# The first stage of a two-layer backbone: a feature tile's eight modulation chunks in one run, and two engine queues in source order

## The chip, the cores and the metric

One core of one Trainium2 chip. The metric is the device time of one execution in microseconds (us), smaller is better. TensorE is called PE below, its weight loads PEld, VectorE DVE, ScalarE ACT, GpSimd POOL; SP is the engine whose queue issues the loads.

## The reference, cut to what matters

Two layers, 512 tokens (256 latent and 256 context), width 2048. Each layer begins with

```python
shift, scale, gate = jnp.split(jax.nn.silu(c) @ w_mod + b_mod, 3, axis=-1)
shift_x, scale_x, gate_x = jnp.split(jax.nn.silu(c_ctx) @ w_mod + b_mod, 3, axis=-1)
z_lat = (rms_norm(h_lat, norm_g) * (1.0 + scale[:, None]) + shift[:, None]) @ w_in
z_ctx = (rms_norm(h_ctx, norm_g) * (1.0 + scale_x) + shift_x) @ w_in
```

and goes on with three branches (a gated linear recurrence, a chunked delta rule, attention), their gates, an output projection and a gated residual. All of it is float32. The two vectors `c` and `c_ctx` are known at the start, but `w_mod` is 2048 x 6144 for each layer, so that the shift and scale of layer 0 have to be computed from 32 MB of weights before the first projection can be fed.

## The kernel before, in words

Features lie on the partitions, tokens along the columns. A feature tile is 128 features; there are 16 (`KT`), and each `Y[k]` holds one tile of the residual for all 512 tokens. A projection in full precision is made of three PE products per feature tile and output tile: both operands are split into a rounded part (`xh`, `wh`) and the rest (`xl`, `wl`), and `accumulate` (L397) issues xh*wh, xh*wl and xl*wh into one PSUM bank.

The change is in the first stage of layer 0, `start_first` (L543). Seven output tiles of the input projection (`NSTART`) are accumulated at once, in seven PSUM banks named pz, pz, pa, pa, pb, pb and pt; the loop runs over the feature tile k outside and over the seven output tiles i inside, so that one k is 21 products of 128x512. Before k can be used, its modulation must be known, and that is what class `Narrow` (L217) does for a tile u:

- `load(u)` (L228) loads the 2048 x 256 columns of `w_mod` that give shift and scale of tile u, as eight chunks in six DMAs: three 256 KB chunks into buffers wb, one into wa, one pair of 512 KB into full or th (in turn), one pair into kq. wb has eight buffers, wa four, kq two, full and th one each, so the last three DMAs of a load reuse what tile u-2 has read.
- `run(u, half)` (L241) multiplies four of the eight chunks with the two vectors: 4 x 4 matmuls with an output of 2x128, each in one of four column strips of the array, all into PSUM tile pm. The trace shows each of them as two records, so the eight chunks are 64 records. After the second half ACT copies pm to SBUF tile s.
- `end(u)` (L251) transposes s with a small matmul against a constant (pm<-sel,s), and DVE makes `modA` and `modS` from it.

`modulate` (L342) then makes u = Y * modA * rb (DVE, two halves), xh (ACT, two halves) and xl (DVE, two halves), where rb is the broadcast of the RMS norm. `first_load` (L521) loads the 448 KB of weights of the seven output tiles for one k into wraw, `first_split` (L525) makes wh (ACT) and wl (DVE) of it. One k thus loads 4 x 256 + 2 x 512 + 448 = 2496 KB.

In the source the first half of tile k+2's chunks stands after output tile 5 of step k, the second half of tile k+1's chunks after output tile 1, `end(k+1)` and `modulate(k+1)` after output tile 2. That is not the order in which PE gets them: the framework's scheduler orders each engine's instructions by its own estimate of when they are ready, and puts pieces of one and two chunks between the products. `late` (L1129, called after k = 11) loads constants that are needed only later.

After the stage, the seven results go to the branches, and `project` (L403) makes the remaining output tiles one by one; small steps of the branches and DVE's own share of the modulation products for later (macc) are put between by a planner that counts estimated engine time. pt is used next by `beta_alpha`.

Of the kernel before, what the change touches and what calls it, by code (L numbers as in the profile page):

```python
# [13 lines left out]
P = 128  # L14
KT = 16
T = 256
TT = 512
# [77 lines left out]
def trunk(ctx, tc, xT, cT, consts, masks, rope_t, small, fg, w_mod0, w_mod, w_first, w_in, w_ba, w_rg, w_out, out):  # L95
    nc = tc.nc
    pe, dve, act, pool = Timed(nc.tensor, "pe"), Timed(nc.vector, "dve"), Timed(nc.scalar, "act"), Timed(nc.gpsimd, "pool")
# [9 lines left out]
    def psum(tag, shape=(P, TT), bufs=2):  # L107
        return ps.tile(list(shape), F32, tag=tag, name=tag, bufs=bufs)
# [3 lines left out]
    def tmp(tag, shape=(P, TT), bufs=None, dt=F32):  # L112
        return wk.tile(list(shape), dt, tag=tag, name=tag, bufs=bufs or BUFS.get(tag, 2))

    def pt_():
        return psum("pt", bufs=1)

    def pa_():
        return psum("pa", bufs=2)

    def pb_():
        return psum("pb", bufs=2)
# [55 lines left out]
    def rsqrt_small(out_, in_, n, add, mul):  # L178
        dve.tensor_scalar(out=out_, in0=in_, scalar1=add, scalar2=mul, op0=ALU.add, op1=ALU.mult)
        pool.tensor_tensor(out=out_, in0=out_, in1=mhalf[:, 0:n], op=ALU.pow)  # L180
# [13 lines left out]
    def rms_bcast(sums, w, between=lambda: None):  # L194
        n = w // P
        p1 = pt_()
        for c in range(n):
            for i, a in enumerate(sums):
                pe.matmul(out=p1[:, 2 * c:2 * c + 2], lhsT=a[:, c * P:c * P + P], rhs=ones[:, 0:2], start=(i == 0), stop=(i == 1))
        r4 = tmp("r4", (P, 8))  # L200
        rsqrt_small(r4[:, 0:n], p1[:, 0:2 * n].rearrange("p (c x) -> p c x", x=2)[:, :, 0], n, 2048.0 * EPS, 1.0 / 2048.0)
        between()
        p2 = pt_()
        for c in range(n):
            pe.matmul(out=p2[:, c * P:c * P + P], lhsT=r4[:, c:c + 1].to_broadcast([P, P]), rhs=ident, start=True, stop=True)
        return p2
# [10 lines left out]
    class Narrow:  # L217
# [20 lines left out]
                w += [two[:, 0], two[:, 1]]  # L238
            self.chunks[u] = w

        def run(self, u, half):  # L241
            for j in range(4 * half, 4 * half + 4):
                for c in range(4):
                    pe.matmul(out=self.pm[32 * c:32 * c + 2, 0:P], lhsT=cs[:, 2 * j + c // 2, :], rhs=self.chunks[u][j][:, c * P:c * P + P],
                              start=(j == 0), stop=(j == 7), tile_position=(0, 32 * c))
            if half:
                self.mt = tmp("s", (P, P))
                act.copy(out=self.mt, in_=self.pm[:, 0:P])
                self.chunks.pop(u)

        def end(self, u):  # L251

# [89 lines left out]
    def modulate(l, k, rb):  # L342
        xr = tmp("u")
        xh[k] = big.tile([P, TT], F32R, tag=f"xh{k}", name=f"xh{k}")
        xl[k] = big.tile([P, TT], F32R, tag=f"xl{k}", name=f"xl{k}")
        half = [slice(T * m, T * m + T) for m in range(2)]
        for m, cc in enumerate(half):
            dve.scalar_tensor_tensor(out=xr[:, cc], in0=Y[k][:, cc], scalar=modA[l][:, k, m:m + 1], in1=rb[:, cc], op0=ALU.mult, op1=ALU.mult)
        for m, cc in enumerate(half):
            act.activation(out=xh[k][:, cc], in_=xr[:, cc], func=AF.Identity, bias=modS[l][:, k, m:m + 1])  # L350
        for m, cc in enumerate(half):
            dve.scalar_tensor_tensor(out=xl[k][:, cc], in0=xr[:, cc], scalar=modS[l][:, k, m:m + 1], in1=xh[k][:, cc].bitcast(F32), op0=ALU.add, op1=ALU.subtract)
# [44 lines left out]
    def accumulate(pz, wh, wl, c0, k, n):  # L397
        a, b = wh[:, c0:c0 + P], wl[:, c0:c0 + P]
        pe.matmul(out=pz[:, 0:n], lhsT=a, rhs=xh[k][:, 0:n], start=(k == 0), stop=False)
        pe.matmul(out=pz[:, 0:n], lhsT=b, rhs=xh[k][:, 0:n], start=False, stop=False)  # L400
        pe.matmul(out=pz[:, 0:n], lhsT=a, rhs=xl[k][:, 0:n], start=False, stop=(k == 15))
# [119 lines left out]
    def first_load(l, k):  # L521
        first_raw[k] = wp.tile([P, 1024], F32, tag="wraw", name="wraw", bufs=4)
        nc.sync.dma_start(out=first_raw[k][:, 0:P * NSTART], in_=w_first[l, k])

    def first_split(k):  # L525
        raw = first_raw.pop(k)
        first_w[k] = [split_w(raw[:, 0:512], 512), split_w(raw[:, 512:P * NSTART], P * NSTART - 512)]
# [15 lines left out]
    def start_first(acc, late):  # L543

        first = [psum("pz"), psum("pz"), pa_(), pa_(), pb_(), pb_()]
        narrow = Narrow()
        for u in range(2):
            narrow.load(u)  # L550
            first_load(0, u)
        pr = rms_bcast(acc, TT, lambda: narrow.run(0, 0))
        rb = tmp("wa")
        dve.tensor_copy(rb, pr)
        narrow.run(0, 1)
        narrow.end(0)
        modulate(0, 0, rb)
        first_split(0)
        narrow.load(2)
        first_load(0, 2)  # L560
        first.append(pt_())
        for k in range(KT):
            for i in range(NSTART):
                wh, wl = first_w[k][i // 4]
                accumulate(first[i], wh, wl, P * (i % 4), k, TT)
                if k + 1 == KT:
                    continue
                if k == 0 and i == 0:
                    narrow.run(1, 0)
                if i == 1:  # L570
                    narrow.run(k + 1, 1)
                    if k + 3 == KT - 1:
                        first_load(0, k + 3)
                    if k + 3 < KT:
                        narrow.load(k + 3)
                    if k + 3 < KT - 1:
                        first_load(0, k + 3)
                    first_split(k + 1)
                if i == 2:
                    narrow.end(k + 1)  # L580
                    modulate(0, k + 1, rb)
                if i == 5 and k + 2 < KT:
                    narrow.run(k + 2, 0)
            first_w.pop(k)
            if k == KT - 5:
                late()
        return first

    def start_layer(l, acc, bs, wide):

        first = [psum("pz"), psum("pz"), pa_(), pa_(), pb_(), pb_()]
        pr = rms_bcast(acc, TT, lambda: [mod_step(pe) for _ in range(FILL)])
        rb = tmp("wa")
        modulate(l, 0, pr)
        dve.tensor_copy(rb, pr)
        first.append(pt_())
        for k in range(KT):
            if k + 1 < KT:
                first_weights(l, k + 1)
                modulate(l, k + 1, rb)  # L600
            for i in sorted(range(NSTART), key=lambda i: wide(TILES[l][i][0])):
                wh, wl = first_w[k][i // 4]
                accumulate(first[i], wh, wl, P * (i % 4), k, TT if wide(TILES[l][i][0]) else T)
            first_w.pop(k)
        return first

    def layer(l, acc, bs):
        last = l == 1
        s = sm[l]
# [7 lines left out]
        def rope_tables():  # L617
            for dst, o in ((cq, 0), (sq_, T)):
                nc.sync.dma_start(out=dst, in_=rope_t[:, o:o + T])
                dve.tensor_scalar(out=dst, in0=dst, scalar1=s[:, S_QN:S_QN + 1], scalar2=None, op0=ALU.mult)  # L620
# [514 lines left out]
        if last:  # L1135
            rope_tables()
            first = start_layer(l, acc, bs, wide)
        else:
            first = start_first(acc, late)
        tiles = TILES[l][NSTART:]  # L1140
        groups = [[t] for t in tiles]
        weights = Weights([[w_in[l, n]] for n in range(len(tiles))] + [[w_out[l, n]] for n in range(KT)])
# [19 lines left out]
        acc = []  # L1162
# [21 lines left out]
    acc = []  # L1184
    for k in range(KT):
        square_into(acc, Y[k], k, TT, dve)
    gw = []
    acc = layer(0, acc, None)
    mod_finish(((1, 0), (1, 1)))
    acc = layer(1, acc, gw[0])  # L1190
    pr = rms_bcast(acc, T)
    rb = tmp("wa")
# [84 lines left out]
```

## Time and profile before

| | us |
|---|---|
| three runs, lowest, median, highest | 1553.96, 1554.66, 1558.1 |
| the profiled execution's own time | 1552.67 |
| its span from the first to the last instruction | 1550.9 |
| mean granted PE clock (1 is 2.4 GHz) | 0.994 |
| PE, PEld, DVE, ACT, POOL busy share of the span | 96%, 77%, 75%, 48%, 7% |

The profiled execution is 1.77 us longer than its span, and 1.99 us below the median of the three runs. Busy time of PE counts a matmul from its start to its modelled end, and these overlap; the pace of PE is read from the distance of two starts.

### The profile page before, as it was taken

The numbers are of one execution on the slowest core, as the hardware profiler recorded it, in microseconds if no ns is written. First come the engines' busy times: TensorE is split into PE (matmuls) and PEld (weight loads), VectorE is DVE, ScalarE is ACT, GpSimd is POOL, SyncE is SP. The second block draws the span as 40 slices with busy tenths as digits, with TensorE's granted clock in tenths as the row PEclk, the third lists the DMA queues.
The fourth block names the chain that finished last, engine by engine and source line by source line (L and its number), as shares of the span: only waits on it lengthen the run. The fifth ranks groups of instructions, "written<-read, shape, count | busy, mean of one in ns | idle before, by whom it ended". The sixth has DMA issues, their size and how long they took to land.

```text
span 1550.9 us, 29964 instructions
## 1 busy us (share of the span) xinstructions
PE 1482.8 (96%) x11762; PEld 1197.9 (77%) x11762; DVE 1164.5 (75%) x2513; ACT 739.3 (48%) x1708; POOL 112.2 (7%) x114
## 2 busy tenths in 40 slices
PE   4999999999999999999999999999999999999996
PEld 2555677787877887788888887967977889779996
DVE  4333888898898888999838776887895676778755
ACT  3222444554544544665422223554544556677653
POOL 0000010100020010000001110010100100000011
PEclk9999999999999999999999999999999999999998
DMA  9888354343443454344436656545662333233663
GB/s 340 286 288 297 111 166 147 97 150 123 143 150 123 150 153 136 97 143 162 135 125 212 204 194 208 174 150 164 198 188 65 96 110 102 76 110 119 194 184 116
DMA packets 90686, 247.68 MB, mean 160 GB/s; under 512 B 9200, under 2 KB 20912, under 8 KB 90544
## 3 DMA queue, kind: packets, MB, share of 16 engines
q1 hardware_dynamic: 89392, 244.71, 49.0%
q8 instruction: 92, 1.51, 0.4%
q10 hardware_dynamic: 1152, 1.05, 0.2%
q14 instruction: 50, 0.41, 0.1%
HBM read 243.60 MB, written 2.13 MB: 158 GB/s over the span
## 4 chain that ended last, share of the span: by engine, by line
PE 76%; DVE 13%; DMA 4%; ACT 4%; issue 2%; POOL 1%; SPq 0%; DVEq 0%; ACTq 0%; POOLq 0%
PE pz L89 54%; PE pa L89 9%; PE pb L89 7%; PE pt L89 3%; PE pm L89 3%; DVE wl L89 3%; DVE wb L89 2%; DVE macc L89 2%; DMA wraw<-in_w_in 1%; DVE u L89 1%; DVE th L89 1%; DMA wb<-in_w_mod 1%; ACT wb L89 1%; ACT wh L89 1%; DMA Y<-in_xT 1%
## 5 line engine op out<-in xcount | busy, mean ns | idle before, releaser
L89 PE MATMUL pz<-xh,wh 128*128 128x512 f32 (+1 forms) x1760 | 645.6, 367 | 8.6 <-ACT xh L89 8.4
L89 PE MATMUL pz<-xh,wl 128*128 128x512 f32 (+1 forms) x1760 | 630.7, 358 | 1.0 <-DVE wl L89 1.0
L89 PE MATMUL pz<-xl,wh 128*128 128x512 f32 (+1 forms) x1760 | 628.7, 357 | 0.0
L89 ACT CAST wh<-wraw 128x512 fp32r<-128x512 f32 x488 | 293.5, 612 | 336.0 <-PE pz L89 212.5
L89 DVE TENSOR_TENSOR wl<-wraw,wh 128x512 fp32r<-128x512 f32 x488 | 328.9, 682 | 134.6 <-ACT wh L89 132.8
L89 PEld LDWEIGHTS pz<-xh,wh 128*128 128x128 f32 x1760 | 331.8, 189 | 58.5 <-ACT xh L89 12.4
L89 PEld LDWEIGHTS pz<-xl,wh 128*128 128x128 f32 x1760 | 332.0, 189 | 50.0 <-issue 2.9
L89 PEld LDWEIGHTS pz<-xh,wl 128*128 128x128 f32 x1760 | 332.5, 189 | 43.2 <-DVE wl L89 1.7
L89 DVE SCALAR_TENSOR_TENSOR macc<-wm,cs,macc 128x512 f32<-128x512 f32 x400 | 293.4, 766 | 1.7 <-DMA wm<-in_w_mod 1.2
L89 PE MATMUL pb<-wb 128*128 128x128 f32 (+1 forms) x560 | 112.5, 328 | 3.9 <-ACT wb L89 2.1
L89 PEld LDWEIGHTS pb<-wb 128*128 128x128 f32 x560 | 79.6, 190 | 17.0 <-ACT wb L89 7.1
L89 DVE TENSOR_SCALAR modA<-pm,nb,small 128x2 f32<-128x2 f32 x16 | 4.5, 279 | 92.5 <-PE pm L89 92.5
L89 ACT ACTIVATE wb<-pb,mx,rqa 128x512 f32<-128x512 f32 (+1 forms) x48 | 33.9, 706 | 42.8 <-DVE mx L89 42.5
L89 POOL TENSOR_TENSOR o<-o,t 128x512 f32<-128x512 f32 (+1 forms) x28 | 30.5, 1089 | 325.6 <-ACT t L89 325.6
L89 DVE SCALAR_TENSOR_TENSOR u<-zp,small,u 128x512 f32<-128x512 f32 (+1 forms) x72 | 50.5, 702 | 2.1 <-ACT u L89 1.8
L89 ACT COPY s<-pm 128x128 f32<-128x128 f32 x16 | 4.2, 265 | 97.1 <-PE pm L89 97.1
L89 ACT ACTIVATE t<-pt 128x128 f32<-128x128 f32 (+1 forms) x122 | 34.1, 279 | 28.9 <-PE pt L89 26.8
L89 ACT ACTIVATE xh<-u,modS 128x256 fp32r<-128x256 f32 x64 | 30.5, 504 | 32.8 <-DVE u L89 32.6
L89 PEld LDWEIGHTS pa<-c,s 32*32 32x32 f32 x2304 | 24.9, 107 | 21.9 <-issue 11.9
L89 DVE TENSOR_REDUCE mx<-pb 128x1 f32<-128x512 f32 (+1 forms) x48 | 28.7, 599 | 10.2 <-PE pb L89 9.9
L89 ACT COPY wb<-pb 128x512 f32<-128x512 f32 (+1 forms) x48 | 24.7, 515 | 22.0 <-PE pb L89 21.4
L89 POOL TENSOR_TENSOR rqa<-rqa,mhalf 128x4 f32<-128x4 f32 (+1 forms) x16 | 17.3, 1083 | 243.7 <-DVE rqa L89 243.7
(260 smaller groups left out, 1811.7 us busy)
## 6 DMA issues: line engine op xcount, KB each, us to landing
wraw<-in_w_in SPq DMA_DIRECT2D x148, 512.0 KB, 3.6
wm<-in_w_mod SPq DMA_DIRECT2D x128, 512.0 KB, 3.8
wraw<-in_w_out SPq DMA_DIRECT2D x64, 512.0 KB, 4.3
wraw<-in_w_first SPq DMA_DIRECT2D x32, 448.0 KB, 5.3
wb<-in_w_mod SPq DMA_DIRECT2D x48, 256.0 KB, 6.5
kq<-in_w_mod SPq DMA_DIRECT2D x16, 512.0 KB, 5.6
Y<-in_xT SPq DMA_DIRECT2D x16, 256.0 KB, 5.3
wa<-in_w_mod SPq DMA_DIRECT2D x16, 256.0 KB, 6.7
```

What stands on the lines that cost most here:

```text
L89: return f(*args, **kw)
```

## The change

`Narrow.run` takes all eight chunks of a tile at once. Its one call per step stands after output tile 1, the calls for the first half are gone, and so is the one inside the RMS norm. `start_first` is called under `manual_schedule` for PE and SP: in that stage these two engines get their instructions in the order of the source; ACT, DVE and POOL are ordered by the scheduler as before.

```diff
-        def run(self, u, half):
-            for j in range(4 * half, 4 * half + 4):
+        def run(self, u):
+            for j in range(8):
                 for c in range(4):
                     pe.matmul(out=self.pm[32 * c:32 * c + 2, 0:P], lhsT=cs[:, 2 * j + c // 2, :], rhs=self.chunks[u][j][:, c * P:c * P + P],
                               start=(j == 0), stop=(j == 7), tile_position=(0, 32 * c))
-            if half:
-                self.mt = tmp("s", (P, P))
-                act.copy(out=self.mt, in_=self.pm[:, 0:P])
-                self.chunks.pop(u)
+            self.mt = tmp("s", (P, P))
+            act.copy(out=self.mt, in_=self.pm[:, 0:P])
+            self.chunks.pop(u)
...
-        pr = rms_bcast(acc, TT, lambda: narrow.run(0, 0))
+        pr = rms_bcast(acc, TT)
...
-        narrow.run(0, 1)
+        narrow.run(0)
...
-                if k == 0 and i == 0:
-                    narrow.run(1, 0)
                 if i == 1:
-                    narrow.run(k + 1, 1)
+                    narrow.run(k + 1)
...
-                if i == 5 and k + 2 < KT:
-                    narrow.run(k + 2, 0)
...
-            first = start_first(acc, late)
+            with tc.manual_schedule(engines={mybir.EngineType.PE, mybir.EngineType.SP}):
+                first = start_first(acc, late)
```

What it does to PE's queue around the end of step k = 1 and the begin of step k = 2 (xh_500 and xl_501 are tile 2 before, xh_502 and xl_503 after; pm<-wb, wa, th, full and kq are modulation chunks, here of tile 3, and pt, pz, pa, pb the projection's products; a row's x4 or x8 counts matmuls). Before:

```order
L89 MATMUL pt<-xh_411,wl 128x512
L89 MATMUL pm<-wb,cs 2x128 x4
L89 MATMUL pt<-xl_412,wh 128x512
L89 MATMUL pm<-wb,cs 2x128 x4
L89 MATMUL pm<-wa,cs 2x128 x4
L89 MATMUL pz<-xh_500,wh 128x512
L89 MATMUL pz<-xh_500,wl 128x512
L89 MATMUL pm<-wb,cs 2x128 x4
L89 MATMUL pz<-xl_501,wh 128x512
```

Now, the same place of PE's queue:

```order
L89 MATMUL pz<-xh_502,wl 128x512
L89 MATMUL pz<-xl_503,wh 128x512
L89 MATMUL pm<-wb,cs 2x128 x8
L89 MATMUL pm<-wa,cs 2x128 x4
L89 MATMUL pm<-wb,cs 2x128 x4
L89 MATMUL pm<-th,cs 2x128 x8
L89 MATMUL pm<-kq,cs 2x128 x8
L89 MATMUL pa<-xh_502,wh 128x512
L89 MATMUL pa<-xh_502,wl 128x512
L89 MATMUL pa<-xl_503,wh 128x512
L89 MATMUL pm<-sel_121,s 128x4
```

The chunks, which before stood in four to six pieces in a step (by PE's whole list 64 pieces for the 13 tiles 2 to 14, 5 for tile 1, 3 for tile 15), are one piece now, and no chunk stands any more ahead of the first product pz<-xh of a step; three products stand between the chunks and the transposing matmul pm<-sel. SP's order of loads in the stage is the same before and now.

PE's queue at the start, in the RMS norm of tile 0 (pt<-cst,r is the broadcast of the norm). Before:

```order
L89 MATMUL pm<-wb,cs 2x128 x4
L89 MATMUL pt<-cst,r_263 128x128
L89 MATMUL pm<-wb,cs 2x128 x4
L89 MATMUL pt<-cst,r_263 128x128
L89 MATMUL pm<-wa,cs 2x128 x4
```

Now:

```order
L89 MATMUL pt<-cst,r_265 128x128 x4
L89 MATMUL pm<-wb,cs 2x128 x8
L89 MATMUL pm<-wa,cs 2x128 x4
L89 MATMUL pm<-wb,cs 2x128 x4
L89 MATMUL pm<-full,cs 2x128 x8
```

All of tile 0's chunks stand behind the broadcast now.

DVE's queue at the end of the stage (the second u is that of a convolution after the stage, Y<-t,pt the gate that empties PSUM bank pt). Before:

```order
L89 MEMSET pm 128x512
L89 SCALAR_TENSOR_TENSOR u<-zp,small_73,u 128x512 x2
L89 TENSOR_TENSOR wl<-wraw,wh 128x512
L89 SCALAR_TENSOR_TENSOR u<-zp,small_73,u 128x512
L89 TENSOR_SCALAR macc<-wm,cs 128x512
L89 SCALAR_TENSOR_TENSOR Y_1701<-t,pt 128x512
```

Now:

```order
L89 SCALAR_TENSOR_TENSOR u<-zp,small_73,u 128x512
L89 TENSOR_SCALAR macc<-wm,cs 128x512
L89 SCALAR_TENSOR_TENSOR u<-zp,small_73,u 128x512
L89 TENSOR_TENSOR wl<-wraw,wh 128x512
L89 SCALAR_TENSOR_TENSOR u<-zp,small_73,u 128x512
L89 TENSOR_SCALAR macc<-wm,cs 128x512
L89 SCALAR_TENSOR_TENSOR macc<-wm,cs,macc 128x512
L89 SCALAR_TENSOR_TENSOR Y_1704<-t,pt 128x512
```

Two more macc steps stand ahead of the gate that empties pt. Later on the five lists differ in a few exchanged neighbours on PE, DVE, ACT and SP up to about a tenth of their length, and not at all after that.

## Rows read from the trace of the kernel before

**Rows 1.** Waits, 0 to 210 us: engine, tile, releaser: us in total, times, longest.
```profile
ACT s L89 <- PE pm L89: 97.1, 16, 11.3
...
PEld pm L89 <- issue: 19.9, 56, 0.7
...
PE pz L89 <- ACT xh L89: 8.4, 11, 1.8
...
PE pm L89 <- DMA wb<-in_w_mod: 0.4, 1, 0.4
```

**Rows 2.** Timeline of PE, first product of steps 0, 1, 14, 15: start us, us.
```profile
32.68 0.53 PE L89 MATMUL pz<-xh,wh 128*128 128x512 f32 x1 [0.71 <-ACT xh L89]
...
43.64 0.50 PE L89 MATMUL pz<-xh,wh 128*128 128x512 f32 x1 [0.88 <-ACT xh L89]
...
157.44 0.51 PE L89 MATMUL pz<-xh,wh 128*128 128x512 f32 x1
...
167.82 0.50 PE L89 MATMUL pz<-xh,wh 128*128 128x512 f32 x1 [1.83 <-ACT xh L89]
```

**Rows 3.** Timeline of PE in step 13, a piece of 16 chunk records between products.
```profile
151.96 0.40 PE L89 MATMUL pa<-xh,wh 128*128 128x512 f32 x1
152.19 0.40 PE L89 MATMUL pa<-xh,wl 128*128 128x512 f32 x1
152.52 0.62 PE L89 MATMUL pm<-full,cs 128*2 128x128 f32 x16
153.07 0.50 PE L89 MATMUL pa<-xl,wh 128*128 128x512 f32 x1
153.41 0.39 PE L89 MATMUL pa<-xh,wh 128*128 128x512 f32 x1
```

**Rows 4.** Timeline of PE and ACT: 48 chunk records of tile 15 in one piece.
```profile
163.73 0.40 PE L89 MATMUL pm<-wa,cs 128*2 128x128 f32 x8
...
164.60 0.62 PE L89 MATMUL pm<-kq,cs 128*2 128x128 f32 x16
165.29 0.27 ACT L89 COPY s<-pm 128x128 f32<-128x128 f32 x1 [6.67 <-PE pm L89]
```

**Rows 5.** Timeline of ACT, PE, DVE: from tile 4's copy s to step 4's first product.
```profile
57.37 0.27 ACT L89 COPY s<-pm 128x128 f32<-128x128 f32 x1 [4.99 <-PE pm L89]
...
57.80 0.28 PE L89 MATMUL pm<-sel,s 128*128 128x4 f32 x2
58.12 0.28 DVE L89 TENSOR_SCALAR modA<-pm,nb,small 128x2 f32<-128x2 f32 x1 [5.22 <-PE pm L89]
...
58.84 1.15 DVE L89 TENSOR_TENSOR wl<-wraw,wh 128x512 fp32r<-128x512 f32 x2
...
60.98 0.50 PE L89 MATMUL pz<-xh,wh 128*128 128x512 f32 x1
```

**Rows 6.** Stretches: us, busy PE PEld DVE ACT POOL, granted clock, DMA share, GB/s.
```profile
27.00:32.00 5.00, 3.48 (x54) 1.97 (x52) 1.71 (x6) 1.48 (x4) 0.00 (x0) 1.00 1.04 391
33.00:36.00 3.00, 3.00 (x21) 0.93 (x20) 0.94 (x3) 0.00 (x0) 0.00 (x0) 0.50 1.03 385
...
74.00:82.00 8.00, 8.00 (x83) 4.53 (x86) 3.06 (x8) 2.10 (x5) 0.00 (x0) 1.00 0.92 315
162.00:170.00 8.00, 5.78 (x79) 3.94 (x79) 3.68 (x9) 2.83 (x7) 0.00 (x0) 1.00 0.16 60
186.00:194.00 8.00, 8.00 (x36) 6.48 (x35) 8.00 (x22) 1.98 (x4) 0.00 (x0) 1.00 0.54 168
```

**Rows 7.** DMA issues, 0 to 165 us: count, KB each, median us to landing.
```profile
kq<-in_w_mod SPq DMA_DIRECT2D x16, 512.0 KB, 5.6
```

**Rows 8.** Timeline after the stage, DVE's gate and PE's first use of pt.
```profile
173.91 0.68 DVE L89 SCALAR_TENSOR_TENSOR Y<-t,pt 128x512 f32<-128x512 f32 x1
...
174.65 0.41 PE L89 MATMUL pt<-xh,kv 128*32 128x512 f32 x1
```

**Rows 9.** Costliest groups of the page: DVE's macc, busy us, mean ns of one, idle before.
```profile
L89 DVE SCALAR_TENSOR_TENSOR macc<-wm,cs,macc 128x512 f32<-128x512 f32 x400 | 293.4, 766 | 1.7 <-DMA wm<-in_w_mod 1.2
```

## The prediction, made before the changed kernel ran

> **What bounds the kernel now.** I read the waits of the first 210 us first, then PE's timeline of the stage by steps, then single pieces of it, and the stretches for loads and clock last. In the waits the reader is to see that ACT and DVE stand still for PE, not the other way round: ACT waits 97.1 us in 16 waits for the chunk matmuls in pm, while PE's products wait 8.4 us in all for ACT's xh, and PE waits for a chunk's load only 0.4 us [rows 1]. The stage is PE's. Its pace is read from the first product of each step: step 1 starts at 43.64 and step 14 at 157.44, so 13 steps take 113.8 us, **8.75 us each**; step 0 takes 10.96 and step 14 takes 10.38 [rows 2].
>
> What fills 8.75 us? Two products stand 0.23 us apart (151.96 to 152.19), so 21 of them are 4.83 us. A piece of 16 chunk records moves the next product from 0.23 to 0.88 us behind the last, and the one after that comes at 0.34 instead of 0.23: 0.76 us for the piece [rows 3]. In a long piece 32 records go by in 0.87 us (163.73 to 164.60), 0.027 us each [rows 4]. So 16 records are 0.435 us, and **0.325 us of every piece is the way in and out**. The wait list says the same from another side: PE's weight loads for pm wait 56 times for nothing that the profile shows, 19.9 us in all or 0.355 each [rows 1]. With 64 pieces for 13 tiles, a step has 4.9 pieces: 4.83 for products, 1.74 for 64 records, 1.6 for entries and exits, some 0.23 (taken as one product's place) for the transposing matmul, 8.4 in all. The rest, 0.35, is the wait for xh.
>
> **The change part by part.** *Pieces.* One piece a step instead of 4.9 takes away 51 pieces in 13 steps, 16.6 us at 0.325. But the chunk matmuls also filled the time in which PE has nothing else, ahead of a step's first product; the next part says what comes late in their place.
>
> *The new step, from the first product at T.* Six products: the sixth starts at T + 0.34 + 4 x 0.23 = T + 1.26. The piece starts 0.33 later (as 152.19 to 152.52 [rows 3]), at T + 1.59. From a 48-record piece's start to the copy s are 1.56 us (163.73 to 165.29 [rows 4]); 16 more records make it 1.99, so s starts at T + 3.58. From s to the next step's first product are 3.61 us now (57.37 to 60.98 [rows 5]): copy, transposing matmul, modA and modS, half of u, two wl, the other half of u, xh. DVE's order in a step stays so. What is new in that chain is that three products stand ahead of the transposing matmul. The records end 0.255 us before s (164.60 + 0.435 against 165.29 [rows 4]) and the next product starts 0.115 after their end [rows 3], so the three start at s - 0.14, s + 0.20 and s + 0.43, and the transposing matmul at s + 0.66, where it was s + 0.43 (57.80 [rows 5]): 0.23 later. The next step starts at T + 3.58 + 3.61 + 0.23 = **T + 7.42**. PE itself would be ready at 4.83 + 1.74 + 0.325 + 0.23 = 7.13. So the chain is the bound by 0.3 us, and it is almost hidden. I take 7.5, a little above, since the third product of a step (xl) now follows at once on the second, with no chunk between, and DVE makes xl behind xh. Ends of the range: 7.1 (PE alone) and 8.0 (below).
>
> *Loads.* A step loads 2496 KB, 2.556 MB; in 7.5 us that is 341 GB/s. In this stage 391 GB/s were moved while the queue was full [rows 6], a floor of 6.5 us. The loads for tile u+2 are freed by the piece of tile u and needed two steps later, 15 us; a 512 KB load lands 5.6 us after its issue [rows 7]. What is queued on SP behind a load that waits for the piece are the weights of the seven tiles and the next tile's chunks, which have a step more. SP's order is unchanged, so that part of the change costs and gives nothing, and I take nothing for loads. The Trainium skill (SBUF — State Buffer, "The DMA setup-cost knee") puts loads of 1 MiB at 330 to 340 GB/s; by that the step would be some 7.6 us and the kernel some 2 us slower than my sum. The 391 GB/s of the trace are above it, and the measurement decides.
>
> *The sum, against the profiled execution's 1552.67 us.*
> - Steps 1 to 13: 13 x (8.75 - 7.5) = -16.3.
> - Step 0 (10.96): PE ran at half clock, 0.50 granted or 1.2 GHz, from 33 to 36 us [rows 6]. I keep its whole excess over 8.75, 2.2 us, and take -1.25. Ends: -3.4 if the slow stretch goes, +0.9 if there is a second one at the same price.
> - Step 14 (10.38): PE waited 1.83 us for xh of tile 15, whose chunks came last of all [rows 2, 4]. It becomes a step like the others: -2.9.
> - Before step 0: tile 0's chunks move behind the norm's broadcast. Three pieces fewer are -1.0; eight records that used a gap now stand on the path, +0.6 at most. I take -0.4, between -1.0 and +0.6.
> - After the stage: PE's first use of pt (174.65) comes right after DVE's gate has emptied it (173.91 + 0.68 [rows 8]), and two more macc steps of up to 0.77 us [rows 9] now stand ahead of that gate, while other work there has moved behind it. I take +0.6, between 0 and 1.5. What stands behind on PE are products that have their data.
> - The exchanged neighbours after that: 0, since they are the same instructions; the next stage keeps its order, so I let the gain arrive at the end in full.
>
> Together -20.25: 1532.4 us for the profiled execution. The median of the runs is 1.99 us above the profiled one, so **1534.4 us**.
>
> **The rivals.** *The loads become the bound* (chance 0.12). For: in the loop the rate stays near 315 GB/s even with the DMA engines 0.92 busy [rows 6], and buffers are now freed in one burst, not piece by piece. Against: the 391 above, and hardly a wait for a load [rows 1]. At 315 GB/s a step is 8.11 us; 14 steps x 0.61 = 8.5 us less gain, 1542.9.
>
> *The chain comes out longer* (0.11). The first product waits for a chain through four engines that was partly covered by chunk matmuls. If half a us is added to it (DVE's xl of the last tile or an ACT cast in front), a step is 8.0, and the gain falls by 14 x 0.5 = 7: 1541.4. For: ACT and DVE have an order set by estimates. Against: 3.61 us were measured with that very order [rows 5].
>
> *The gain is given back after the stage* (0.06). DVE is busy for the whole of 186 to 194 us [rows 6]; if later loads or its work, not PE, set the pace there, the time stays near 1553 to 1555. Against: PE is busy through the same stretch.
>
> *Slower, by the clock* (0.05). PE ran at half clock in step 0, after a stretch (27 to 32 us) in which it was busy 3.48 of 5 us with chunks for the most part [rows 6]. If a 64-record piece in every step brings the clock down, each step pays step 0's 2.2 us: 14 x 2.2 = 30.8 against a gain of 20.25, 1565 us. It decides from 1.45 us a step on (20.25 / 14). Against it: 162 to 170 us held a 48-record piece and 1.83 us of standing still, and the clock granted was 1.00 [rows 2, 4, 6]. The Trainium skill (TensorE: Matmul & The Clock Gate, "Part 1: The HAM clock gate") says that half clock is the default and that recent activity releases the full one; the trace agrees, PE was busy in all of 33 to 36 us before the clock rose; what a piece in every step does no run here shows.
>
> That the change does not do what it says is ruled out for PE by its list, and is what I expect for SP's part.
>
> **How the numbers follow.** My forecast has 0.66, the rivals 0.12, 0.11, 0.06 and 0.05. A difference under 0.3%, 4.7 us here, can't be told from no change. The forecast and the first two rivals are faster by more: 0.89, less 0.01 for mixtures of them; the third is no change, 0.07 with that; slower 0.05. The range: the low end is my sum with part of the better step (7.1 would give another 14 x 0.4 = 5.6, that is 1528.8; I stop at 1530); the high end takes in both faster rivals, 1544.
>
> **What would show it.** Right: steps of 7.3 to 7.6 us between first products, one piece with one wait of some 0.35 us a step, the sum of waits for "issue" of pm near 5 us instead of 19.9, a wait of PE for xh of about 0.2 to 0.3 us in each step, loads at about 340 GB/s from 45 us on, step 15 near 147 us instead of 167.82, and the stages after it as long as before. Wrong: waits of pm for loads (first rival), steps near 8 with long waits for xh (second), a later stage that has grown by what the first lost (third), a granted clock under 1 between 45 and 147 us (fourth).

## The result, and the profile after

The changed kernel takes **1532.74 us**, the median of four runs (1529.33 to 1534.94); the kernel before took 1554.86 beside it (four runs, 1553.96 to 1558.1). The ratio is 0.9852, 95% interval 0.9829 to 0.9876. Forecast were 1534.4 us, from 1530 to 1544. The profiled execution took 1529.33 us, its span is 1527.5; it is the fastest of the four. In a second set, with an execution of 1531.91 us in the profile, the changed kernel had a median of 1532.45 against 1557.5 (0.985, 0.9828 to 0.9872).

The waits of the changed kernel, 0 to 190 us (engine, tile, releaser: us in total, times, longest), which answer to [rows 1]:

```profile
ACT s L89 <- PE pm L89: 67.0, 16, 10.1
...
PEld pz L89 <- ACT xh L89: 8.6, 15, 2.5
...
PEld pm L89 <- issue: 5.6, 15, 0.7
...
PE pz L89 <- ACT xh L89: 2.4, 1, 2.4
...
PEld pm L89 <- DMA wb<-in_w_mod: 0.4, 1, 0.4
```

ACT still waits for PE, 67.0 us instead of 97.1. The weight loads for pm wait 15 times for nothing that is shown, 5.6 us instead of 19.9: one piece a step. PE's weight loads for pz wait in every step for xh: 15 times, 8.6 us, of which 2.5 are ahead of step 0, so 0.43 in each of the other 14; its products themselves show only the wait ahead of step 0 (2.4 us, where they waited 8.4 us in 11 waits before [rows 1]). No chunk is waited for in the steps.

The first products of steps 0, 1, 14 and 15, in PE's timeline of the changed kernel (start us, us), which answer to [rows 2]:

```profile
31.24 0.80 PE L89 MATMUL pz<-xh,wh 128*128 128x512 f32 x1 [2.43 <-ACT xh L89]
...
41.44 0.50 PE L89 MATMUL pz<-xh,wh 128*128 128x512 f32 x1
...
138.78 0.50 PE L89 MATMUL pz<-xh,wh 128*128 128x512 f32 x1
...
146.09 0.39 PE L89 MATMUL pz<-xh,wh 128*128 128x512 f32 x1
```

Steps 1 to 13 take 97.34 us, **7.49 each**, where they took 113.8. Step 0 takes 10.20 (10.96), step 14 takes 7.31 (10.38), and step 15 begins 21.73 us earlier (167.82).

One step and the begin of the next, timeline of ACT, PE and DVE of the changed kernel, which answers to [rows 4, 5]:

```profile
82.52 0.27 ACT L89 COPY s<-pm 128x128 f32<-128x128 f32 x1 [3.70 <-PE pm L89]
...
83.17 0.28 PE L89 MATMUL pm<-sel,s 128*128 128x4 f32 x2
83.49 0.28 DVE L89 TENSOR_SCALAR modA<-pm,nb,small 128x2 f32<-128x2 f32 x1 [4.15 <-PE pm L89]
...
84.20 1.16 DVE L89 TENSOR_TENSOR wl<-wraw,wh 128x512 fp32r<-128x512 f32 x2
...
85.79 0.51 ACT L89 ACTIVATE xh<-u,modS 128x256 fp32r<-128x256 f32 x1 [0.96 <-DVE u L89]
86.35 0.50 PE L89 MATMUL pz<-xh,wh 128*128 128x512 f32 x1
...
88.00 0.62 PE L89 MATMUL pm<-wb,cs 128*2 128x128 f32 x16
...
90.00 0.27 ACT L89 COPY s<-pm 128x128 f32<-128x128 f32 x1 [3.70 <-PE pm L89]
```

With T = 86.35 the piece starts at T + 1.65, s at T + 3.65, 2.00 behind the piece's start; from s to the next first product are 3.83 us (82.52 to 86.35). The two together are the step, as they must be; that it is the chain behind s for which the step waits is seen at its end: the second xh ends at 86.30 (85.79 + 0.51), 0.05 us ahead of the product that uses it.

Stretches of the changed kernel (us, then busy time of PE, PEld, DVE, ACT and POOL, granted PE clock, DMA share, GB/s), which answer to [rows 6]:

```profile
28.00:32.00 4.00, 1.18 (x8) 0.80 (x4) 3.15 (x9) 2.10 (x5) 0.00 (x0) 0.80 1.05 387
32.00:36.00 4.00, 4.00 (x46) 2.50 (x48) 0.50 (x2) 0.00 (x0) 0.00 (x0) 0.50 1.04 388
40.00:80.00 40.00, 39.99 (x447) 29.27 (x446) 17.45 (x44) 11.59 (x26) 0.00 (x0) 1.00 0.97 337
80.00:120.00 40.00, 40.00 (x503) 29.54 (x502) 15.73 (x40) 11.13 (x26) 0.00 (x0) 1.00 0.97 344
```

In the steps the loads run at 337 to 344 GB/s and the granted clock is 1.00. Step 0 still has a stretch at 0.50.

After the stage a little is lost. PE's waits where the branches begin, before (190 to 230 us) and changed (170 to 210 us):

```profile
PE pt L89 <- ACT t L89: 1.7, 1, 1.7
PE pt L89 <- DVE wb L89: 0.7, 1, 0.7
PE pt L89 <- DVE kv L89: 0.5, 1, 0.5
```

```profile
PE pt L89 <- DVE wb L89: 1.5, 1, 1.5
PE pt L89 <- ACT t L89: 1.4, 1, 1.4
PE pt L89 <- DVE kv L89: 0.7, 1, 0.7
PE pt L89 <- ACT u L89: 0.4, 1, 0.4
```

They were 2.9 us and are 4.0. A load that both kernels issue there, wa<-rows_d, is at 293.74 before and at 273.34 in the changed kernel: of the 21.73 us that the stage gained 20.40 are left, and 1.1 of the missing 1.3 are these waits. What the one profiled execution gains beyond that, 3.0 us up to its end (1550.9 - 1527.5 = 23.4), is not there in the profile of the second set (a span of 1530.1, 20.8 us less): it lies within the spread of the runs.

### The profile page after: what moved, and what is told of

It reads as the page before. It is cut to its first block, busy times and chain, and to the rows that moved or that the text cites. A ratio compares the mean times of both kernels' runs of the same rounds, so it can differ in the third digit from the quotient of the medians.

```text
span 1527.5 us, 29952 instructions
## 1 busy us (share of the span) xinstructions
PE 1466.9 (96%) x11762; PEld 1206.4 (79%) x11762; DVE 1165.8 (76%) x2513; ACT 739.9 (48%) x1708; POOL 113.2 (7%) x114
## 4 chain that ended last, share of the span: by engine, by line
PE 82%; DVE 10%; ACT 3%; DMA 2%; issue 1%; POOL 1%; SPq 0%; DVEq 0%; ACTq 0%; POOLq 0%
PE pz L89 58%; PE pa L89 9%; PE pb L89 8%; PE pt L89 4%; PE pm L89 3%; DVE wb L89 2%; DVE wl L89 1%; DVE macc L89 1%; DMA wraw<-in_w_in 1%; DVE th L89 1%; DVE o L89 1%; ACT t L89 1%; ACT wb L89 1%; DMA wa<-rows_d 1%; DVE u L89 1%
```

## The experiments

T is the start of a step's first product; "s at" and "chain" (from s to the next first product) are read in the middle of the stage, the step is the mean over the steady part. The ratio is to the kernel before on the same chip.

| kernel | pieces a step | products ahead of the last piece | s at | chain | step | median, ratio (95%) |
|---|---|---|---|---|---|---|
| before | 4.9 | 12, 13 or 15 | T + 4.93 to 6.17 | 3.61 (3.24 where it is not the bound) | 8.75 | 1554.86 |
| merge_only | 4.2 | 12, 13 or 15 | T + 4.91 to 6.38 | 3.62 (2.92 where it is not the bound) | 8.73 | 1553.51, 0.9991 (0.9974 to 1.0007) |
| four_pieces | 4 | 6 | T + 2.93 | not the bound | 8.10 | 1541.12, 0.9918 (0.9902 to 0.9934) |
| one_late | 1 | 12 | T + 5.03 | 2.78 | 7.82 | 1539.47, 0.9905 (0.989 to 0.9919) |
| split2 | 2 | 6 | T + 3.95 | 3.85 | 7.80 | 1537.07, 0.9878 (0.9853 to 0.9903) |
| after | 1 | 6 | T + 3.65 | 3.83 | 7.49 | 1532.74, 0.9852 (0.9829 to 0.9876) |
| order_only | 2 | 6 | T + 2.61 | not the bound | 7.47 | 1535.51, 0.9872 (0.9847 to 0.9896) |
| late | 1 | 9 | T + 4.32 | 2.98 | 7.30 | 1533.27, 0.986 (0.9834 to 0.9885) |
| early | 1 | 3 | T + 2.79 | not the bound | 7.154 | 1528.96, 0.9826 (0.9801 to 0.9852) |
| early_fill | 1 | 3 | as early | not the bound | 7.154 | 1525.26, 0.9799 (0.9775 to 0.9824) |

### Which half of the change does it: order_only and merge_only

order_only, against before, has the queues fixed and keeps the two halves:

```diff
+            with tc.manual_schedule(engines={mybir.EngineType.PE, mybir.EngineType.SP}):
+                first = start_first(acc, late)
```

> Before's source, with the halves of a tile's chunks still apart (first half after output tile 5 of the step before, second half after output tile 1), but PE's and SP's queues in source order: two pieces of 32 records a step where after has one of 64 and before has 4.9 pieces of various lengths. Theory A (PE's pace is products, records and 0.325 us for each piece, and the chain from s to the next first product is 3.84 us): PE needs 4.83 + 1.74 + 2 x 0.325 + 0.23 = 7.45 us a step, the chain after a piece of only 32 records would be ready at 6.55, so PE is the bound and waits for no xh; steps of 7.4 to 7.6, as in after (7.485), and the time is 1532 us, between 1530 and 1536. Theory B (it is the one run of eight chunks that gives the gain, not the queues' order): steps stay near 8.4 to 8.75 and the time near 1548 to 1554. Theory C (the loads set the 7.5 us): steps 7.5 as well, but with waits of pm for loads.

merge_only, against before, has the one run and no fixed queues:

```diff
-        def run(self, u, half):
-            for j in range(4 * half, 4 * half + 4):
+        def run(self, u):
+            for j in range(8):
...
-                    narrow.run(k + 1, 1)
+                    narrow.run(k + 1)
```

> After without the fixed order: all eight chunks stand in one run in the source, but PE's and SP's queues are ordered by the scheduler, which takes the run apart again: 55 pieces for tiles 2 to 14, 4.2 a step, instead of 13 (after) and 64 (before). Theory A: 4.83 + 1.74 + 4.2 x 0.325 + 0.23 = 8.17 us for PE and some 0.3 of waiting for xh, a step of 8.4 to 8.6; the gain over before is 14 x 0.15 to 14 x 0.35, 2 to 5 us, the time 1549 to 1553 us. Theory B (the one run gives the gain): 1532 to 1536 us.

order_only gave 1535.51 us with steps of 7.47, merge_only 1553.51, which can't be told from before. **It is the fixed order, not the one run**: written as one run, but left to the scheduler, the chunks are taken apart again. Of the two queues it is PE's alone: with only PE's fixed the order of all five engines is that of the changed kernel.

order_only's steps are no longer than after's, yet it is 3 us slower. PE's weight loads wait for a chunk nine times, which was not expected, without a longer step. Its waits, 0 to 180 us:

```profile
PEld pm L89 <- DMA kq<-in_w_mod: 3.6, 9, 0.7
```

Step 15 begins at 145.38 there, 0.7 us earlier than in after, and wa<-rows_d is at 274.34, 1.0 later: 1.7 of the 3 us are lost between. In that piece PE stands still 2.5 us for t instead of 1.4, and then runs slower, by the stretches of order_only:

```profile
188.00:192.00 4.00, 1.98 (x8) 1.69 (x9) 3.34 (x10) 3.71 (x16) 2.24 (x3) 0.79 0.10 20
192.00:196.00 4.00, 4.00 (x17) 3.22 (x16) 3.44 (x11) 2.94 (x10) 0.08 (x1) 0.78 0.57 190
```

Where the rest of the 3 us lies was not looked for; the interval of the ratio overlaps with after's.

merge_only missed theory A's steps of 8.4 to 8.6, and its time lies 0.5 us above the range that theory A gave. Nine pieces fewer in 13 tiles should have given 0.23 us a step, and gave 0.02. Where they went is in its waits of 0 to 180 us:

```profile
PEld pm L89 <- issue: 18.3, 50, 0.7
...
PE pz L89 <- ACT xh L89: 10.2, 12, 1.8
```

Waits without a reason fell by 1.6 us (19.9 [rows 1]), and PE's waits for xh rose by 1.8 (8.4 [rows 1]). PE and ACT in merge_only show why, with the step that begins at 86.81:

```profile
86.81 0.50 PE L89 MATMUL pz<-xh,wh 128*128 128x512 f32 x1 [1.09 <-ACT xh L89]
...
91.29 0.62 PE L89 MATMUL pm<-kq,cs 128*2 128x128 f32 x16
...
91.97 0.27 ACT L89 COPY s<-pm 128x128 f32<-128x128 f32 x1 [5.21 <-PE pm L89]
...
95.59 0.50 PE L89 MATMUL pz<-xh,wh 128*128 128x512 f32 x1 [0.62 <-ACT xh L89]
```

The last piece, kq, stands behind 13 products; s comes at T + 5.16, the chain takes 3.62, and PE waits for xh at its end: the step is 8.78, however many pieces there are. In before it is the same: in the step that begins at 52.43 the last piece stands behind 12 products, s is at T + 4.94 and the next first product 3.61 later [rows 5], a step of 8.55. Other steps of before are longer: from step 3 on they repeat in threes, some 8.80, 8.17 and 9.77 us, and the longest of the three has its last piece behind 15 products. PE and ACT of before, the step that begins at 104.69:

```profile
104.69 0.50 PE L89 MATMUL pz<-xh,wh 128*128 128x512 f32 x1
...
110.14 0.62 PE L89 MATMUL pm<-kq,cs 128*2 128x128 f32 x16
...
110.83 0.27 ACT L89 COPY s<-pm 128x128 f32<-128x128 f32 x1 [6.87 <-PE pm L89]
...
114.44 0.51 PE L89 MATMUL pz<-xh,wh 128*128 128x512 f32 x1 [1.09 <-ACT xh L89]
```

Here s is at T + 6.14, and the chain takes 3.61 again. The step of 8.17 ahead of it ends without a wait for xh, which is ready 0.73 us earlier: PE's own queue sets that one. In merge_only the three are 8.78, 7.87 and 9.99 (the means of 8.75 and 8.73 take in all steps from 1 to 13): fewer pieces take 0.30 off the step that PE sets, and the next gives 0.22 of it back, since s comes at T + 6.37 in it. That made a new theory (F): a step is the larger of two things, PE's own sum, in which pieces count, and the place of s plus the chain behind it.

### A second piece, and the place of the one: split2, early, late

split2:

```diff
+                if i == 0:
+                    narrow.run(k + 1, range(4))
                 if i == 1:
-                    narrow.run(k + 1)
+                    narrow.run(k + 1, range(4, 8))
```

> After, with the run split in the middle by one output tile: chunks 0 to 3 after output tile 0, chunks 4 to 7 after output tile 1, everything else where it was. One more piece in each step, no instruction more. Theory A: a second way in and out of 0.325 us a step; PE then needs 7.45 us, the second piece begins no earlier, s comes at about T + 3.9 less the 0.87 us that the first 32 records take ahead plus those 0.87 ahead of the later product, so about 0.3 later than in after (2.00 us behind the piece's start there), and as the chain from s sets the step, the step grows to 7.75 to 7.8; 14 x 0.3 = 4 us more than after, 1535.5 to 1538 us. If a piece costs nothing by itself (the cost before was the waiting for chunks or for xh), the time is that of after within 1.5 us.

Measured: 1537.07 us, steps of 7.80, s at T + 3.95. One more piece is 0.31 us more in each step, and all of it arrives.

early (the loads and the split of weights that stand beside the run move with it, here and in late and one_late):

```diff
-                if i == 1:
+                if i == 0:
                     narrow.run(k + 1)
...
-                if i == 2:
+                if i == 1:
                     narrow.end(k + 1)
```

> After, with the run one output tile earlier (after output tile 0 instead of 1) and the transposing matmul with what follows also one earlier (after output tile 1 instead of 2). s and the chain behind it come 0.69 us earlier in each step (three products). Theory A (the chain of 3.84 us behind s ends last in after, by 0.3 to 0.4 us): the next xh is ready before PE gets to it, PE waits for it no more, and a step is PE's own 7.13 to 7.2 us; 14 x 0.3 = 4 us less than after, 1527 to 1530 us, loads at 357 GB/s. Theory C (the loads hold the step at 7.5): steps stay at 7.45 to 7.5, PE waits for chunks in pm instead of for xh, and the time is that of after within 1.5 us. Theory D (ACT and DVE, not the order on PE, hold the step): also 7.45 to 7.5, with xh still awaited.

Measured: 1528.96 us. The waits of early, 0 to 190 us, have no wait for xh left but that ahead of step 0:

```profile
PEld pz L89 <- ACT xh L89: 2.5, 1, 2.5
```

Its steps are 7.154 us from step 1 on, which is PE's own sum (7.13 by the prediction's terms). No chunk is waited for in them, at 359 GB/s from 80 to 120 us. So the loads did not bound the changed kernel's 7.49 (theory C falls), and neither ACT nor DVE by themselves (theory D): it was the chain behind s, by 0.33 us a step. In early and in split2 DVE's order within the chain is that of after, so these two move the place of s alone.

late:

```diff
-                if i == 1:
+                if i == 2:
                     narrow.run(k + 1)
...
-                if i == 2:
+                if i == 3:
                     narrow.end(k + 1)
```

> After, with the run one output tile later (after output tile 2) and the transposing matmul after output tile 3 instead of 2. s comes 0.69 us later in each step. Theory A (the chain from s to the next first product ends last): each step grows by 0.69 us less what DVE's other order takes out of the way (the two wl go behind u and xl, 1.08 us less ahead of xh), but then PE's second product of a step waits for wl; a step of 7.8 to 8.2 us, 14 x 0.3 to 14 x 0.7 or 4 to 10 us more, 1537 to 1543 us. If PE's own pace or the loads set the step, the place of the run does not matter and the time is that of after within 1.5 us.

Measured: 1533.27 us, no difference from after, but with two steps of 8.18 (1 and 2), then 7.30. The expectation of 4 to 10 us more was a miss, and by its last sentence theory A would fall. The steady steps tell otherwise; timeline of late, ACT and PE:

```profile
99.41 0.27 ACT L89 COPY s<-pm 128x128 f32<-128x128 f32 x1 [3.87 <-PE pm L89]
...
102.39 0.50 PE L89 MATMUL pz<-xh,wh 128*128 128x512 f32 x1
```

The chain is 2.98 us instead of 3.83. The scheduler, which still orders DVE, put both wl out of the middle of u's two halves, and PE did not have to wait for them. s came 0.67 later and the chain is 0.85 shorter: 7.30 instead of 7.49. The place of s mattered, but another term moved with it; the equal time comes from four longer steps (0, 1, 2 and 14) and eleven shorter ones.

### Number of pieces against place of the last: four_pieces and one_late

four_pieces starts from order_only and cuts its two pieces in two:

```diff
-            for j in range(4 * half, 4 * half + 4):
+            for j in range(2 * part, 2 * part + 2):
...
+                if i == 0:
+                    narrow.run(k + 1, 2)
                 if i == 1:
-                    narrow.run(k + 1, 1)
+                    narrow.run(k + 1, 3)
...
+                if i == 4 and k + 2 < KT:
+                    narrow.run(k + 2, 0)
                 if i == 5 and k + 2 < KT:
-                    narrow.run(k + 2, 0)
+                    narrow.run(k + 2, 1)
```

> Fixed order of PE and SP with the chunks of a tile in four pieces of two (before had 4.9), the last of them where after has its one: tile k+2's first two pieces after output tiles 4 and 5 of step k, tile k+1's last two after output tiles 0 and 1 of it. The last piece holds 16 records, so s comes at about T + 3.1 (T + 3.66 in after) and the chain, 3.84, would allow a step of 6.95. Theory F (a step is the larger of PE's own sum and of the place of s plus the chain behind it; pieces count in PE's sum with 0.31 each): PE's sum is 7.155 + 3 x 0.31 = 8.09 us, no wait for xh, 14 x 0.6 = 8.4 us more than after, 1539 to 1543 us. Theory G (before lost its time by the place of the last chunk alone, which stood behind 12 or 13 products of the step, and pieces cost nothing that is seen): steps of 7.2 to 7.5 and 1528 to 1533 us.

one_late:

```diff
-                if i == 1:
+                if i == 3:
                     narrow.run(k + 1)
...
-                if i == 2:
+                if i == 4:
                     narrow.end(k + 1)
```

> After, with its one piece behind 12 products of a step (after output tile 3), where the scheduler of before has the last of its pieces, and the transposing matmul after output tile 4. Theory F: s comes six products later, at T + 3.66 + 6 x 0.23 = T + 5.04; DVE's order has the two wl behind xl here, as in the late kernel, so the chain is 2.76 to 2.98 us instead of 3.83, and a step is 7.8 to 8.0 us though it has one piece only; each step's first product waits 0.6 to 0.9 us for xh; 14 x 0.3 to 14 x 0.5, 4 to 7 us more than after, 1536.5 to 1540 us. Theory H (the number of pieces alone sets the step): 7.15 to 7.3 us as in the early and the late kernel, 1528 to 1533 us.

Both came out by theory F: 1541.12 us with steps of 8.10 (8.09 expected), and 1539.47 us with steps of 7.82 (7.8 to 8.0). In four_pieces s comes at T + 2.93 and PE never waits for xh in a step, but its pieces cost it 0.95 us a step, 0.317 for each of the three more than in early. In one_late there is one piece, and the step is 0.66 longer than PE's sum, by place and chain. (Its product waits 0.33 to 0.34 us for xh, where 0.6 to 0.9 were expected.) Timeline of one_late, PE and ACT:

```profile
97.25 0.50 PE L89 MATMUL pz<-xh,wh 128*128 128x512 f32 x1 [0.34 <-ACT xh L89]
...
101.60 0.62 PE L89 MATMUL pm<-kq,cs 128*2 128x128 f32 x16
102.28 0.27 ACT L89 COPY s<-pm 128x128 f32<-128x128 f32 x1 [4.17 <-PE pm L89]
105.06 0.50 PE L89 MATMUL pz<-xh,wh 128*128 128x512 f32 x1 [0.33 <-ACT xh L89]
```

The kernel before had both against it: by 0.315 a piece PE's sum was some 7.154 + 3.9 x 0.315 = 8.38 in the mean (an estimate), and place and chain gave 8.55 to 9.79 in the steps that they set. Taking away one of the two gives a part of the 22 us: four_pieces, with the place of after, is 13 us faster than before, one_late, with the one piece, 14.6. But one_late's chain is also 0.83 us shorter (2.78 instead of 3.61), since DVE's order moved with the place, and its place no longer changes from step to step; what the pieces alone would give behind 12 products was not measured. The change lowered both.

### The start, and a version faster than both: after_again, early_fill, fill_only, early_fill2

after_again is the changed kernel, measured beside the next ones:

> The changed kernel once more, so that the others of this call have it on the same chip: 1532.7 us, between 1530 and 1535, with steps of 7.485 us.

Measured: 1532.45 us (1531.91 to 1533.55), steps of 7.50.

early_fill puts tile 1's chunks ahead of the loop in early:

```diff
         first_split(0)
+        narrow.run(1)
...
                 if i == 0:
-                    narrow.run(k + 1)
+                    if k:
+                        narrow.run(k + 1)
```

> The early kernel (run after output tile 0, transposing matmul after output tile 1), and tile 1's chunks moved ahead of the loop, into the time in which PE waits 2.4 us for xh of tile 0. Theory A: step 0 then has no chunk piece in it, 1.74 + 0.325 = 2.1 us less for PE, and the wait of 2.4 us is filled instead; since the chunks of tile 1 must have landed and pm be free by then, I expect 1.5 to 2.1 us of it: 1524 to 1528 us. If the start is bound by something else (the loads of tile 1, or the slow clock between 31 and 37 us), it is that of the early kernel within 1 us.

Measured: **1525.26 us**, 7.2 less than the changed kernel on the same chip. Against early it is more than the 1.5 to 2.1 us that were expected in the stage: step 1 begins at 37.94 instead of 41.50. To see why, fill_only does the same in the changed kernel:

> After, with tile 1's chunks ahead of the loop (in the 2.4 us in which PE waits for xh of tile 0) and nothing else moved: the runs of the other tiles stay after output tile 1, the transposing matmul after output tile 2. Theory E (PE drops to half clock at 32 us because it stood still at 28 to 31 us, and step 0 pays for that): with the wait filled the granted clock stays 1.00 as in the early kernel with the same filling, step 0 is 21 products without a chunk, 5.2 us, and step 1 begins near 38 us instead of 41.3 to 41.44; steps of 7.485 after that; 3.3 us less than after, 1528 to 1530 us. If the half clock has another cause (it comes at that time of the start whatever PE does), step 0 keeps its slow stretch, only the 1.74 + 0.325 us of the chunks move into the wait, and the time is 1530.5 to 1532 us.

Measured: 1530.2 us (0.9831, 0.981 to 0.9852); step 0 takes 5.22 us and step 1 begins at 38.35. PE's timeline of fill_only:

```profile
27.47 1.08 PE L89 MATMUL pm<-full,cs 128*2 128x128 f32 x16
28.33 1.08 PE L89 MATMUL pm<-kq,cs 128*2 128x128 f32 x16
...
31.27 0.62 PE L89 MATMUL pm<-wb,cs 128*2 128x128 f32 x16 [1.10 <-DVE modS L89]
31.71 0.40 PE L89 MATMUL pm<-wa,cs 128*2 128x128 f32 x8
...
33.13 0.50 PE L89 MATMUL pz<-xh,wh 128*128 128x512 f32 x1
33.47 0.39 PE L89 MATMUL pz<-xh,wl 128*128 128x512 f32 x1
33.70 0.39 PE L89 MATMUL pz<-xl,wh 128*128 128x512 f32 x1
```

And its stretches:

```profile
28.00:32.00 4.00, 2.52 (x58) 1.64 (x54) 1.79 (x6) 1.55 (x4) 0.00 (x0) 1.00 1.04 388
32.00:36.00 4.00, 4.00 (x57) 3.27 (x50) 3.38 (x10) 1.75 (x5) 0.00 (x0) 1.00 1.04 384
```

The first product comes 1.0 to 1.9 us later than in the changed kernel (32.10 and 31.24 in its two profiles), since the chunks have to wait until modS has read pm. But the half clock is gone from step 0: the column shows 1.00, 16 chunk records go by in 0.44 us from 31.27 on, and step 0's products stand 0.23 us apart. All ten profiles without the filling, that of before among them, have a stretch at 0.50 between 30 and 38 us, and the three with it have none. So theory E holds: step 0 paid for PE's standing still ahead of it. The gain is 3.0 us up to step 1. The median lies 2.3 below that of after_again, which was measured in another set, and 0.2 above the expected range.

early_fill2 is early_fill again:

> The early kernel with tile 1's chunks ahead of the loop, a second time, beside the one above on the same chip: 1525 us, between 1522 and 1527, steps of 7.155 us, granted clock 1.00 from 28 to 40 us, 3 to 5 us less than the kernel above (14 x 0.33 = 4.6 by the steps, less what the branches after the stage give back).

Measured: **1525.36 us** (0.9797, 0.9777 to 0.9817), 4.8 less than fill_only on the same chip, as the steps say (14 x 0.33 = 4.6).

## Why the prediction was right, and which of its steps were not

**Pieces.** The cost of a piece was right: 0.325 us forecast, 0.31 to 0.32 measured in three ways (split2, order_only, four_pieces). What it was used for was not. "One piece a step instead of 4.9 takes away 51 pieces in 13 steps, 16.6 us" reads as if this were the gain, with the wait for xh as a remainder of 0.35. merge_only shows that pieces taken away turn into waits for xh as long as the last chunk stands late and the chain keeps its length. The wait was the sign that the chain bound most of the steps before as well, and besides taking pieces away the change moved the last chunk from behind 12 to 15 products to behind 6. That 16.6 lies so near the 16.46 that steps 1 to 13 gained is luck: by the estimate above the old step was 0.37 longer than PE's own sum (8.75 against 8.38), and the new one is 0.33 longer than its own (7.49 against 7.154), so that the two excesses cancel.

**The new step.** Here the prediction worked with the right mechanism, so that its sum held: piece at T + 1.59 (T + 1.65), s 1.99 behind it (2.00), the chain 3.84 (3.83), PE's own sum 7.13 (7.154 in early), the step 7.42 and 7.5 taken (7.49). The 0.06 by which the piece is late has the cause for which 7.42 was raised to 7.5: behind the first xl product (86.92) the next comes 0.29 us later, where products otherwise stand 0.23 apart. Steps 1 to 13: -16.3 forecast, 97.34 - 113.8 = -16.46 measured.

**Loads.** Taken at nothing, rightly: no chunk was waited for in the steps at 337 to 344 GB/s, and early moved 359 without a wait. That rules the first rival out. The second rival (a longer chain, steps of 8.0 us) did not come in after; one_late, at 7.82, shows that the chain can set such a step, there by the place of the piece.

**The start.** Step 0: -1.25 forecast, -0.76 measured; before it: -0.4 forecast, -1.44 measured. Together -1.65 against -2.20: step 0 still paid for a stretch at half clock. In the second profile of the changed kernel the two are -1.76 and -0.58, so how they divide changes from run to run. These are the terms that were sized worst, and fill_only took 3.0 us from them. The fourth rival, that this price is paid in every step, did not happen: the clock was 1.00 from 40 us on.

**Step 14**: -2.9 forecast, 7.31 - 10.38 = -3.07 measured, as a step like the others, with no wait ahead of step 15.

**After the stage**: +0.6 forecast at the first use of pt, where PE has no wait now; instead about 1.3 are lost between 178 and 273 us, mostly in the branches' small steps. The place was wrong, the size near, within the ends of 0 to 1.5. The third rival is out: what the stage gained arrived at the end.

The sum by 273 us is -20.40, against a forecast of -20.25. That it is so near is in part luck: 0.55 more was gained at the start and 0.33 more in steps 1 to 14, and 0.73 more was lost after the stage. The other term of the median, that it lies some 2 us above the profiled execution, did not carry over: it is 3.4 above it here.

## What to carry to other kernels

When an engine looks full but a short wait stands ahead of each round, ask first where in the round the last input of the next round's chain is made: the round is that place plus the chain, and filling the engine better does nothing for such a round until the place is moved or the chain shortened. Then count what is left of the engine's own sum, kind of work by kind of work, and the cost of each change between kinds. A gap ahead of a long dense stretch is worth filling with work from inside it twice over, if the engine runs slower after it has stood still.

## What the runs showed of the hardware

**A switch between the 4-strip chunk matmuls and the full-array products costs 0.31 to 0.32 us each time it is made and undone**, beyond the 0.027 us of each record, whether one piece of 64 records is made two of 32 (order_only, split2) or four of 16 (four_pieces). The Trainium skill (TensorEngine Tiling (Array Packing), "Key Properties") says that changing the tiling mode drains the engine; it gives no time, and the runs here agree with a fixed price per switch. They don't show that the drain is what is paid.

**The clock after a short stand.** In the changed kernel PE stood still for 2.43 us ahead of step 0 and was busy 1.18 of 4 us from 28 to 32, and the granted clock was 0.50 (1.2 GHz) from 32 to 36; with 64 chunk records put into that stand it was busy 2.52 of 4 us in fill_only, and the clock stayed at 1.00 (2.4 GHz) in step 0, in all three kernels with the filling. The kernel before had 16 of these records in the same place, with waits of 1.10 and 0.71 us around them, and its clock fell to 0.50 at 33 us [rows 2, 6]:

```profile
31.34 0.62 PE L89 MATMUL pm<-wb,cs 128*2 128x128 f32 x16 [1.10 <-DVE modS L89]
```

After the stage the clock fell again in order_only, behind a stand of 2.5 us, and in early_fill2, behind one of 2.02; the changed kernel has 1.36 and 1.5 us there and kept 1.00. The Trainium skill (TensorE: Matmul & The Clock Gate, "Part 1: The HAM clock gate") says that the full clock is released by recent activity, and that the moment at which it comes varies from run to run; the runs agree with both. Tile 0's chunks go by at 16 records in 0.44 us from 26.98 in the first profile of the changed kernel, and still at 16 in 0.85 us from 26.96 in the second, where step 0 took 9.20 us instead of 10.20.

The column of the granted clock doesn't show this: it reads 1.00 from the start in all of these profiles, though 16 records take 0.86 us at 27.47 in fill_only and 0.81 us at 27.59 in the kernel before, the pace of the stretch at 0.50 (0.81 us from 34.09 in the changed kernel). So the 1.00 that [rows 6] give for 27 to 32 us does not stand for the full pace throughout.

**Loads.** early_fill2 moved more than the steps before were thought to allow (a stretch of early_fill2):

```profile
40.00:80.00 40.00, 40.00 (x497) 31.89 (x486) 17.67 (x46) 12.79 (x29) 0.00 (x0) 1.00 1.03 377
```

377 GB/s over 40 us, with PE busy all the time. So the 315 GB/s of the kernel before [rows 6], on which the first rival rested, were no limit of the queue.
